# Rotary embedding on one core: fp32 tiles cast on ScalarE, against bf16 tiles of whole batch rows cast inside GpSimd-queue DMAs

## The chip, the cores and the metric

One core of a Trainium2 chip. The metric is device time in microseconds (us) of the whole program. Engines: DVE is VectorE, ACT is ScalarE, POOL is GpSimd, SP is SyncE; in the traces, DMAs issued from SP are queue q1, from ACT q10 and from GpSimd q0 (software_dynamic, here the software queue), all booked on the same 16 DMA engines (before: q1 50.1% and q10 49.1% of their span). SBUF is the memory of the kernel's tiles. A packet is one record of the DMA trace; here, but for small records of 4 bytes, it is one contiguous row of DRAM (in the kernel before, 29 DMAs of 128 rows of 32 KB are 3712 records).

## The reference

```python
# x: (8, 2048, 16, 64) fp32; cos, sin: (2048, 32) fp32
x1, x2 = x_pairs[..., 0], x_pairs[..., 1]      # neighbouring elements
out1 = x1 * cos - x2 * sin
out2 = x1 * sin + x2 * cos
out  = stack([out1, out2], axis=-1)            # fp32
```

x and out have 67.1 MB each, the two tables 0.5 MB together. So at least 134.7 MB cross the DMA engines, and each element needs three elementwise operations: multiply by sin, multiply by cos, add with the neighbours swapped.

## The kernel before

There are 16 tiles of 128 partitions x 8 seq rows x 1024 elements in fp32 (32 KB per partition, 4 MB per tile), in 5 buffers. ACT casts half a tile to bf16, DVE does three bf16 `tensor_tensor` operations, and ACT casts back to fp32 into the same tile. Loads are issued from SP, stores from ACT. The first and the last tile are cut into smaller runs.

```python
def load(i):
    g, b = groups[i]
    tiles[i] = xpool.tile([P, K, HD], fp32, name="xt")            # 5 buffers
    for k0, k1 in load_runs(i):
        nc.sync.dma_start(out=tiles[i][:, k0:k1], in_=x_t[b, g, :, k0:k1])

def halve(j):
    i, k0, k1 = pieces[j]
    halved[j] = hpool.tile([P, 4, HD], bf16, name="xh", bufs=3)
    nc.scalar.copy(out=halved[j][:, : k1 - k0], in_=tiles[i][:, k0:k1])
# ... rotate(j): three nc.vector.tensor_tensor in bf16 ...
def widen(j):
    i, k0, k1 = pieces[j]
    nc.scalar.copy(out=tiles[i][:, k0:k1], in_=rotated.pop(j)[:, : k1 - k0])
    # ... nc.scalar.dma_start(out=out_t[...], in_=tiles[i][...]) when the tile is complete
    if k1 == K and i + NX < n:
        load(i + NX)                       # SP waits until the store of tile i has landed
```

## Time and profile before

| | before |
|---|---|
| time, median of the runs beside the change | 318.56 us |
| span of the profiled run | 316.93 us |
| DVE busy / ACT busy | 223.2 / 230.0 us |
| bytes read and written in DRAM | 134.7 MB |
| share of 16 DMA engines' span filled by packets of the two big queues | 99.2% |

The profile's page of the kernel before: span; busy time with its share of the span; the busy tenths of each engine in 40 slices and what the DMA engines moved; the queues with packets, MB and share of 16 engines' span; the chain that ended last; then the groups of instructions (busy us, mean ns, idle time before them and what ended it).

```profile
span 316.9 us, 352 instructions
DVE 223.2 (70%) x111; ACT 230.0 (73%) x73; POOL 0.2 (0%) x4
...
DVE  0189999999999596693967939588440999999112
ACT  4078899999998692976949679495803999997322
...
DMA  7999999999999999999999999999999999999997
...
DMA packets 6451, 134.76 MB, mean 425 GB/s; under 512 B 689, under 2 KB 1201, under 8 KB 1969
...
q1 hardware_dynamic: 3712, 67.63, 50.1%
q10 hardware_dynamic: 2736, 67.11, 49.1%
...
HBM read 67.63 MB, written 67.11 MB: 425 GB/s over the span
...
DMA 62%; ACT 26%; DVE 4%; issue 3%; another core or an unknown queue 2%; SPq 1%; ACTq 1%
...
L75 ACT CAST xh<-xt 128x4096 bf16<-128x4096 f32 (+2 forms) x36 | 116.1, 3224 | 66.9 <-DMA xt<-in_x_dram 61.6
L105 ACT CAST xt<-xh 128x4096 f32<-128x4096 bf16 (+2 forms) x36 | 116.0, 3223 | 14.8 <-DVE xh L100 14.4
L94 DVE TENSOR_TENSOR qt<-xh,s_tab 128x4096 bf16<-128x4096 bf16 (+2 forms) x36 | 74.0, 2055 | 71.2 <-ACT xh L75 70.3
...
L121 DVE CAST s_tab<-sin_sb 128x512 bf16<-128x512 f32 x1 | 0.5, 453 | 14.4 <-DMA sin_sb<-in_sin_dram 14.4
```

Both compute engines are idle for over a quarter of the span, and what they wait for leads back to loads. The DMA row is 9 from the second slice to the last but one. That ACT holds 26% of the chain that ended last does not make it a bound: the chain walks through one instruction at a time, and during nearly every ACT cast on it the DMA engines were full as well.

The trace's packet records are sharper than the slices: 27.2 bytes per ns is the slope between the 16 KB packet (611 ns) and the 32 KB packet (1213 ns), loads and stores alike. 134.74 MB at 16 x 27.2 bytes/ns take 309.6 us. So the kernel before spends only 7.3 us of its span on anything but moving bytes at that rate.

### The profile page before, as it was taken

How to read it: one execution, taken by the hardware profiler on the slowest of the kernel's cores; microseconds unless marked ns; L12 is line 12 of the kernel's file. 1: busy time of each engine (PE TensorE's matmuls, PEld its weight loads, DVE VectorE, ACT ScalarE, POOL GpSimd, SP SyncE). 2: the span in 40 equal slices, each digit the busy share in tenths (PEclk: the TensorE clock that was granted, in tenths of full speed). 3: DMA queues.
4: the chain of work that ended last, by engine and by line, in shares of the span. 5: the costliest groups of instructions: out<-in, count | busy, mean ns of one | idle time of the engine just before them, and what ended most of it. 6: DMA issues, size and time to landing. Idle time of an engine off the chain costs nothing.

```text
span 316.9 us, 352 instructions
## 1 busy us (share of the span) xinstructions
DVE 223.2 (70%) x111; ACT 230.0 (73%) x73; POOL 0.2 (0%) x4
## 2 busy tenths in 40 slices
DVE  0189999999999596693967939588440999999112
ACT  4078899999998692976949679495803999997322
POOL 0000000000000000000000000000000000000000
DMA  7999999999999999999999999999999999999997
GB/s 304 424 463 405 455 397 401 459 438 422 455 405 463 397 460 401 459 414 448 443 418 455 405 459 405 455 405 459 418 443 447 414 428 430 424 433 439 442 414 302
DMA packets 6451, 134.76 MB, mean 425 GB/s; under 512 B 689, under 2 KB 1201, under 8 KB 1969
## 3 DMA queue, kind: packets, MB, share of 16 engines
q1 hardware_dynamic: 3712, 67.63, 50.1%
q10 hardware_dynamic: 2736, 67.11, 49.1%
q14 instruction: 3, 0.02, 0.0%
HBM read 67.63 MB, written 67.11 MB: 425 GB/s over the span
## 4 chain that ended last, share of the span: by engine, by line
DMA 62%; ACT 26%; DVE 4%; issue 3%; another core or an unknown queue 2%; SPq 1%; ACTq 1%
DMA xt<-in_x_dram 31%; DMA out_dram<-xt 28%; ACT xt L105 14%; ACT xh L75 12%; DMA sin_sb<-in_sin_dram 4%; DVE xh L100 1%; DVE xh L95 1%; DVE qt L94 1%; SPq L70 1%; ACTq L109 1%; DVE s_tab L121 0%; SPq L115 0%; DVE s_tab L122 0%; ACTq L105 0%
## 5 line engine op out<-in xcount | busy, mean ns | idle before, releaser
L75 ACT CAST xh<-xt 128x4096 bf16<-128x4096 f32 (+2 forms) x36 | 116.1, 3224 | 66.9 <-DMA xt<-in_x_dram 61.6
L105 ACT CAST xt<-xh 128x4096 f32<-128x4096 bf16 (+2 forms) x36 | 116.0, 3223 | 14.8 <-DVE xh L100 14.4
L94 DVE TENSOR_TENSOR qt<-xh,s_tab 128x4096 bf16<-128x4096 bf16 (+2 forms) x36 | 74.0, 2055 | 71.2 <-ACT xh L75 70.3
L100 DVE TENSOR_TENSOR xh<-xh,qt 128x4096 bf16<-128x4096 bf16 (+2 forms) x36 | 74.0, 2055 | 1.2
L95 DVE TENSOR_TENSOR xh<-xh,c_tab 128x4096 bf16<-128x4096 bf16 (+2 forms) x36 | 74.0, 2055 | 1.2
L121 DVE CAST s_tab<-sin_sb 128x512 bf16<-128x512 f32 x1 | 0.5, 453 | 14.4 <-DMA sin_sb<-in_sin_dram 14.4
L75 ACT ACT_TABLE_LOAD x1 | 1.3, 1283 | 0.7 <-PEq L147 0.7
L123 DVE CAST c_tab<-cos_sb 128x1024 bf16<-128x1024 f32 x1 | 0.7, 684 | 0.0
L122 DVE TENSOR_SCALAR s_tab<-sin_sb 128x512 bf16<-128x512 f32 x1 | 0.4, 442 | 0.0
L147 POOL MEMSET const-bfloat16-1.0<- 128x1 bf16 x1 | 0.1, 101 | 0.0
L147 POOL MEMSET const-uint8-127<- 128x1 uint8 x1 | 0.1, 101 | 0.0
L147 POOL MEMSET const-float32-0.0<- 128x1 f32 x1 | 0.1, 98 | 0.2 <-issue 0.2
L147 POOL MEMSET const-float32-1.0<- 128x1 f32 x1 | 0.1, 98 | 0.0
## 6 DMA issues: line engine op xcount, KB each, us to landing
out_dram<-xt ACTq DMA_DIRECT2D x15, 4096.0 KB, 38.6
xt<-in_x_dram SPq DMA_DIRECT2D x14, 4096.0 KB, 26.6
xt<-in_x_dram SPq DMA_DIRECT2D x2, 2048.0 KB, 16.3
xt<-in_x_dram SPq DMA_DIRECT2D x4, 512.0 KB, 24.1
xt<-in_x_dram SPq DMA_DIRECT2D x2, 1024.0 KB, 19.9
out_dram<-xt ACTq DMA_DIRECT2D x1, 2048.0 KB, 17.6
out_dram<-xt ACTq DMA_DIRECT2D x1, 1024.0 KB, 11.7
out_dram<-xt ACTq DMA_DIRECT2D x2, 512.0 KB, 4.1
```

The source lines that it names most:

```text
L70: nc.sync.dma_start(out=tiles[i][:, k0:k1], in_=x_t[b, g, :, k0:k1])
L75: nc.scalar.copy(out=halved[j][:, : k1 - k0], in_=tiles[i][:, k0:k1])
L94: nc.vector.tensor_tensor(out=rows(qt), in0=rows(xh), in1=tab(s_tab), op=mult)
L95: nc.vector.tensor_tensor(out=rows(xh), in0=rows(xh), in1=tab(c_tab), op=mult)
L100: nc.vector.tensor_tensor(out=xh3, in0=xh3, in1=q_swap, op=add)
L105: nc.scalar.copy(out=tiles[i][:, k0:k1], in_=rotated.pop(j)[:, : k1 - k0])
L109: nc.scalar.dma_start(out=out_t[b, g, :, r0:r1], in_=tiles[i][:, r0:r1])
L121: nc.vector.tensor_copy(out=s2[:, :, 0], in_=sin_flat)
L122: nc.vector.tensor_scalar_mul(s2[:, :, 1], sin_flat, -1.0)
L123: nc.vector.tensor_copy(out=c_tab.rearrange("p g k (i j) -> p (g k i) j", j=2), in_=cos_sb.rearrange("p g c -> p (g c)").to_broadcast([P, ...
L147: nc = _bacc.Bacc("TRN2", target_bir_lowering=False, num_devices=1)
```

## The change

The intent: 64 KB DRAM rows instead of 32 KB, hence fewer packets, with halved tiles, so that five of them take as much of SBUF as before, and no casts on ACT. One tile is a batch (128 partitions x 16 seq rows), held in bf16 (32 KB per partition, 5 buffers as before). A load DMA reads fp32 and writes bf16, a store DMA reads bf16 and writes fp32; both are issued from GpSimd. The first 1 MB (HEAD) and the last 2 MB (TAIL) stay fp32 DMAs on SP with a cast on ACT.

```diff
-    K = 8
-    G = S // (P * K)
+    K = S // P              # 16
+    KP = 4
+    HEAD = 2
+    TAIL = 4
...
+    def load(b, k0=0):
+        if b not in tiles:
+            tiles[b] = xpool.tile([P, K, HD], bf16, name="xt")
+        nc.gpsimd.dma_start(out=tiles[b][:, k0:], in_=x_t[b, :, k0:])
+
+    def store(b, k1=K):
+        nc.gpsimd.dma_start(out=out_t[b, :, :k1], in_=tiles[b][:, :k1])
... (halve and widen are gone; rotate works in place on the tile, 4 rows at a time)
+        head = stage.tile([P, TAIL, HD], fp32, name="st")
+        for k in range(HEAD):
+            nc.sync.dma_start(out=head[:, k : k + 1], in_=x_t[0, :, k : k + 1])
         nc.sync.dma_start(out=cos_sb, in_=cos_t)
         nc.sync.dma_start(out=sin_sb, in_=sin_t)
+        load(0, HEAD)
+        for b in range(1, NX):
+            load(b)
...
+        for b in range(B):
+            ... # rotate the pieces of batch b
+            if b < B - 1:
+                store(b)
+            if b >= 1 and b - 1 + NX < B:
+                load(b - 1 + NX)          # one batch later than it could be
+        store(B - 1, K - TAIL)
+        tail = stage.tile([P, TAIL, HD], fp32, name="st")
+        # one element into batch 6's tile: waits until batch 6's store has landed
+        nc.scalar.copy(out=tiles[B - 2][:1, 0, :1], in_=tiles[B - 1][:1, K - 1, :1])
+        nc.scalar.copy(out=tail, in_=tiles[B - 1][:, K - TAIL :])
+        nc.sync.dma_start(out=out_t[B - 1, :, K - TAIL :], in_=tail)
```

More of the change, by code (lines that the diff above doesn't have):

```diff
@@ L31 @@
     NX = 5
-    x_t = x.rearrange("b (g p k) h d -> b g p k (h d)", p=P, k=K)
-    out_t = out.rearrange("b (g p k) h d -> b g p k (h d)", p=P, k=K)
-    cos_t = cos.rearrange("(g p k) c -> p g (k c)", p=P, k=K)
-    sin_t = sin.rearrange("(g p k) c -> p g (k c)", p=P, k=K)
+    HEAD = 2
+    TAIL = 4
+    x_t = x.rearrange("b (p k) h d -> b p k (h d)", p=P, k=K)
+    out_t = out.rearrange("b (p k) h d -> b p k (h d)", p=P, k=K)
+    cos_t = cos.rearrange("(p k) c -> p (k c)", p=P, k=K)
+    sin_t = sin.rearrange("(p k) c -> p (k c)", p=P, k=K)
@@ L39 @@
     consts = ctx.enter_context(tc.tile_pool(name="consts", bufs=1))
     xpool = ctx.enter_context(tc.tile_pool(name="xpool", bufs=NX))
-    hpool = ctx.enter_context(tc.tile_pool(name="hpool", bufs=1))
-    cos_sb = consts.tile([P, G, K * D2], fp32)
-    sin_sb = consts.tile([P, G, K * D2], fp32)
-    c_tab = consts.tile([P, G, K, D], bf16)
-    s_tab = consts.tile([P, G, K, D], bf16)
-    groups = [(g, b) for g in range(G) for b in range(B)]
-    n = len(groups)
-    first_runs = [(0, 1), (1, 2), (2, 4), (4, 8)]
@@ L51 @@
-    last_runs = [(0, 4), (4, 6), (6, 7), (7, 8)]
-    def load_runs(i):
-        return first_runs if i == 0 else last_runs if i == n - 1 else [(0, K)]
-    def store_runs(i):
-        return last_runs if i == n - 1 else [(0, K)]
-    pieces = []
-    for i in range(n):
-        runs = first_runs if i == 0 else last_runs if i == n - 1 else [(0, 4), (4, 8)]
-        pieces += [(i, k0, k1) for k0, k1 in runs]
-    tiles, halved, rotated = {}, {}, {}
-    def load(i):
-        g, b = groups[i]
-        tiles[i] = xpool.tile([P, K, HD], fp32, name="xt")
-        for k0, k1 in load_runs(i):
-            nc.sync.dma_start(out=tiles[i][:, k0:k1], in_=x_t[b, g, :, k0:k1])
@@ L72, in halve @@
-    def halve(j):
-        i, k0, k1 = pieces[j]
-        halved[j] = hpool.tile([P, 4, HD], bf16, name="xh", bufs=3)
-        nc.scalar.copy(out=halved[j][:, : k1 - k0], in_=tiles[i][:, k0:k1])
-    def rotate(j):
-        i, k0, k1 = pieces[j]
-        g, _ = groups[i]
+    qpool = ctx.enter_context(tc.tile_pool(name="qpool", bufs=1))
+    stage = ctx.enter_context(tc.tile_pool(name="stage", bufs=1))
+    cos_sb = consts.tile([P, K * D2], fp32)
+    sin_sb = consts.tile([P, K * D2], fp32)
+    c_tab = consts.tile([P, K, D], bf16)
@@ L80, in rotate @@
+    s_tab = consts.tile([P, K, D], bf16)
+    tiles = {}
+    def load(b, k0=0):
[4 more added lines that the diff above has]
+        nc.gpsimd.dma_start(out=out_t[b, :, :k1], in_=tiles[b][:, :k1])
+    def rotate(b, k0, k1):
         nk = k1 - k0
-        xh = halved.pop(j)
-        qt = hpool.tile([P, 4, HD], bf16, name="qt")
+        xp = tiles[b][:, k0:k1]
+        qt = qpool.tile([P, KP, HD], bf16, name="qt")
@@ L84, in rows @@
         def rows(a):
-            return a[:, :nk].rearrange("p k (h e) -> p k h e", h=H, e=D)
+            return a.rearrange("p k (h e) -> p k h e", h=H, e=D)
         def tab(a):
             return dataclasses.replace(
-                a,
-                offset=a.offset + (g * K + k0) * D,
-                ap=[a.ap[0], [D, nk], [0, H], [1, D]],
-            )
-        nc.vector.tensor_tensor(out=rows(qt), in0=rows(xh), in1=tab(s_tab), op=mult)
-        nc.vector.tensor_tensor(out=rows(xh), in0=rows(xh), in1=tab(c_tab), op=mult)
+                a, offset=a.offset + k0 * D, ap=[a.ap[0], [D, nk], [0, H], [1, D]]
+            )
@@ L96, in rotate @@
+        nc.vector.tensor_tensor(out=rows(qt[:, :nk]), in0=rows(xp), in1=tab(s_tab), op=mult)
+        nc.vector.tensor_tensor(out=rows(xp), in0=rows(xp), in1=tab(c_tab), op=mult)
         q_swap = dataclasses.replace(
@@ L98, in rotate @@
         )
-        xh3 = xh[:, :nk].rearrange("p k (a j) -> p (k a) j", j=2)
-        nc.vector.tensor_tensor(out=xh3, in0=xh3, in1=q_swap, op=add)
-        rotated[j] = xh
-    def widen(j):
-        i, k0, k1 = pieces[j]
-        nc.scalar.copy(out=tiles[i][:, k0:k1], in_=rotated.pop(j)[:, : k1 - k0])
-        g, b = groups[i]
-        for r0, r1 in store_runs(i):
-            if r1 == k1:
-                nc.scalar.dma_start(out=out_t[b, g, :, r0:r1], in_=tiles[i][:, r0:r1])
-        if k1 == K and i + NX < n:
-            load(i + NX)
+        x3 = xp.rearrange("p k (a j) -> p (k a) j", j=2)
@@ L113 @@
+        nc.vector.tensor_tensor(out=x3, in0=x3, in1=q_swap, op=add)
     with tc.manual_schedule():
-        load(0)
+        head = stage.tile([P, TAIL, HD], fp32, name="st")
+        for k in range(HEAD):
+            nc.sync.dma_start(out=head[:, k : k + 1], in_=x_t[0, :, k : k + 1])
         nc.sync.dma_start(out=cos_sb, in_=cos_t)
         nc.sync.dma_start(out=sin_sb, in_=sin_t)
-        for i in range(1, NX):
-            load(i)
-        s2 = s_tab.rearrange("p g k (i j) -> p (g k i) j", j=2)
@@ L120 @@
-        sin_flat = sin_sb.rearrange("p g c -> p (g c)")
-        nc.vector.tensor_copy(out=s2[:, :, 0], in_=sin_flat)
-        nc.vector.tensor_scalar_mul(s2[:, :, 1], sin_flat, -1.0)
+        load(0, HEAD)
+        for b in range(1, NX):
+            load(b)
+        nc.scalar.copy(out=tiles[0][:, :HEAD], in_=head[:, :HEAD])
+        s2 = s_tab.rearrange("p k (i j) -> p (k i) j", j=2)
+        nc.vector.tensor_copy(out=s2[:, :, 0], in_=sin_sb)
+        nc.vector.tensor_scalar_mul(s2[:, :, 1], sin_sb, -1.0)
@@ L123 @@
         nc.vector.tensor_copy(
-            out=c_tab.rearrange("p g k (i j) -> p (g k i) j", j=2),
-            in_=cos_sb.rearrange("p g c -> p (g c)").to_broadcast([P, G * K * D2, 2]),
-        )
-        halve(0)
-        for j in range(len(pieces)):
-            if j + 1 < len(pieces):
-                halve(j + 1)
-            rotate(j)
-            widen(j)
+            out=c_tab.rearrange("p k (i j) -> p (k i) j", j=2),
+            in_=cos_sb.to_broadcast([P, K * D2, 2]),
+        )
+        for b in range(B):
+            if b == 0:
+                rotate(b, 0, HEAD)
+                rotate(b, HEAD, KP)
+            for k0 in range(KP if b == 0 else 0, K, KP):
+                rotate(b, k0, k0 + KP)
+            if b < B - 1:
+                store(b)
+            if b >= 1 and b - 1 + NX < B:
+                load(b - 1 + NX)
```

## The prediction

> **What bounds the kernel now.** The DMA engines. In the page's 40 slices the DMA row is 9 in all but the two end slices. The DMA table gives 134.76 MB at a mean of 425 GB/s; packets of the load queue (50.1%) and the store queue (49.1%) fill 99.2% of 16 engines' span. A 32 KB packet, load or store, takes 1213 ns, a 16 KB one 611 ns: 27.2 bytes per ns and about 8 ns fixed. [...] Counted over time, the engines lose only 4.1 us of 316.9 us, half at each end. In the view of waits DVE waits 70.3 us for ACT, ACT 61.6 us for loads.
>
> **What the change does.**
> - It removes nearly all casts from ACT (230 us busy). They are 26% of the chain of waits, but DMA runs full at the same time, so I count about 0 us for this.
> - DVE work stays: about 32 pieces x 3 x 2.29 us, 223 us.
> - DMA bytes on the DRAM side stay at 134.7 MB; on the SBUF side they are halved. I take it that a cast packet costs what its wider side costs: the engine must still read 4 bytes per element in a load and write 4 in a store at 27.2 bytes/ns, and loads and stores follow each other in one queue in 8 MB blocks, so the idle half of each isn't overlapped.
> - Rows of 64 KB instead of 32 KB: estimate 2409 + 8 ns, against 2 x 1213. Saves about 1.1 us per engine.
> - Estimate per engine: head in 4 KB packets (16 x 159 ns) 2.5 us, cos/sin 1.3, loads 152.3, stores 154.7: 311 us busy, against 312.8 now.
> - Start: head and tables (3.8 us of transfers) cover the start of the software-generated queue. End: the last 6 MB (48 KB rows) and 2 MB (16 KB rows) have 128 rows each in two queues, which end together if they alternate. DVE should be done by about 255 us.
> - [...]
>
> Together: 311 us of transfers + 2 at each end + 1.6 from span to time = 316 us, 0.8% faster.
>
> **What would show it.** DMA row full from end to end; 64 KB packets near 2.42 us in loads and stores; DVE 223 us busy and 90 us idle, waiting for loads; ACT nearly empty; GpSimd's stores long from issue to landing, queued behind loads.
>
> **What would make it wrong.**
> 1. Cast packets priced by the SBUF side or the mean of both: well under 2.4 us per 64 KB. DMA would fall to 160-235 us and DVE (223 us, plus start, last cast and store) would bound it at 240-255 us; a partial gain gives 260-305.
> 2. Cast packets dearer than plain ones: 330 us and beyond.
> 3. Bubbles in the single queue: a load waits for a store of the same buffer to land; with another store queued behind, I expect none.
> 4. An end not balanced between the queues: a few us.
>
> 80% range 292 to 325. Faster by over 2% 0.27, within 2% 0.57, slower by over 2% 0.16.

The sum: 311 + 2 + 2 + 1.6 us, 316.4 with the 310.8 behind the 311, which the text gives as 316; its 1.6 is time less span of the kernel before (318.5 - 316.9). Of the start, the changed kernel's trace shows SP's first packet at 1.7 us, 1.0 us after its issue, and its head packets until 6.0 us; GpSimd's first packet came at 5.1 us, 3.9 us after its issue. Of the end it shows turns of one 16 KB packet (644 ns) and one of the 48 KB rows (1828 ns), but only from 305.8 us on: the GpSimd queue's data ended at 311.1 us, SP's at 314.8.

## The result and the profile after

| | before | after |
|---|---|---|
| time, median | 318.56 us | 317.54 us |
| ratio | | 0.9967, 95% interval 0.995 to 0.9985 |
| span of the profiled run | 316.93 us | 316.01 us |
| ACT busy | 230.0 us | 6.9 us |
| DVE busy | 223.2 us | 221.8 us |

A ratio is the mean time of one kernel's runs over that of the other's in the same rounds, so it is not quite the ratio of the medians. The change is 1.0 us faster where 2.5 us were forecast. Nearly all work of an engine was removed and the time moved by a third of a per cent.

The page of the changed kernel, the same parts, with the DMA issues at its end (KB each on the SBUF side, median us from issue to landing).

```profile
span 316.0 us, 198 instructions
DVE 221.8 (70%) x102; ACT 6.9 (2%) x4; POOL 8.9 (3%) x20
...
DVE  0000039999999999999999999999999999100000
ACT  1200000000000000000000000000000000000400
...
DMA  9899999999999999999999999999999999999996
...
DMA packets 3025, 101.72 MB, mean 322 GB/s; under 512 B 336, under 2 KB 336, under 8 KB 848
...
q0 software_dynamic: 2304, 98.04, 96.8%
q1 hardware_dynamic: 720, 3.67, 3.1%
...
HBM read 67.63 MB, written 67.11 MB: 426 GB/s over the span
...
another core or an unknown queue 91%; DMA 2%; ACTq 1%; ACT 1%; SPq 0%; issue 0%
...
L94 DVE CAST s_tab<-sin_sb 128x512 bf16<-128x512 f32 x1 | 0.5, 453 | 44.2 <-DMA sin_sb<-in_sin_dram 44.2
...
L117 ACT CAST st<-xt 128x4096 f32<-128x4096 bf16 x1 | 3.6, 3599 | 0.0
...
out_dram<-st SPq DMA_DIRECT2D x1, 2048.0 KB, 15.5
st<-in_x_dram SPq DMA_DIRECT2D x2, 512.0 KB, 4.5
cos_sb<-in_cos_dram SPq DMA_DIRECT2D x1, 256.0 KB, 22.4
sin_sb<-in_sin_dram SPq DMA_DIRECT2D x1, 256.0 KB, 42.1
```

How to read it:

- The DMA row is as full as before. The mean of 322 GB/s is a trap: a cast load is recorded with the bytes that it wrote (bf16; 32 KB for a 64 KB row). The line with DRAM bytes shows the true rate, 426 GB/s, as before (425).
- The view of the chain is of no use here. It does not know the GpSimd queue's landings and books 91% as an unknown queue. Packet records carry the argument instead.
- The cast packets cost what their wide side costs. From the packet records (median ns):

```text
packet                            before      after
32 KB fp32 -> 32 KB fp32          1213        -
64 KB fp32 -> 32 KB bf16 (load)   -           2432
32 KB bf16 -> 64 KB fp32 (store)  -           2449
```

So a halved SBUF side buys nothing: 64 KB take 2432 ns in a cast load, 2449 ns in a cast store and 2 x 1213 = 2426 ns in two plain ones. That premise of the prediction held, in loads and in stores.

Recorded durations of neighbouring packets overlap a little (in the changed kernel 64 KB cast loads of 2432 ns start 2413 ns apart on an engine, in the median), so their sums are not exact. A better account is the time in which the engines did not move bytes: for each stretch of the span, its length less (DRAM-side bytes moved in it) / (16 x 27.2 bytes/ns), a cast load counted with twice its recorded bytes. In us:

```text
stretch of the span        0-20   20-100   100-260   260-310   310-end   sum
before                     2.95    1.02     0.81      0.39      2.15     7.32
after                      3.22    0.50     0.57      0.12      1.99     6.40
```

The middle is 1.0 us better, the start 0.3 us worse, the end 0.2 us better. That is the difference of the two spans, 0.9 us.

One thing in the profile was not foreseen. DVE starts at 44 us, not near 10: the sin table, 256 KB, needs 42.1 us from issue to landing. Its packets (2 KB, 96 ns) share each DMA engine with the GpSimd queue's packets, and the records show turn-taking: one 2 KB packet, then one of 2129 or 2431 ns, and so on, with 16 table packets per engine. The 256 table packets start in 16 rounds of 16, about 2204 ns apart beside the packets of 2129 ns and 2505 ns apart beside those of 2431 ns. DVE's end moved too, to 269.4 us, where I had expected 255. DVE's idle time is 44.2 us before the table and 46.6 us after its last piece; the view of waits names no wait for loads. Whether that costs time is tested below.

### The profile page after: what moved, and what is told of

Read it like the earlier page. It is cut to its first block, busy times and chain, and to the rows that moved or that the text cites. A ratio compares the mean times of both kernels' runs of the same rounds, so it can differ in the third digit from the quotient of the medians.

```text
span 316.0 us, 198 instructions
## 1 busy us (share of the span) xinstructions
DVE 221.8 (70%) x102; ACT 6.9 (2%) x4; POOL 8.9 (3%) x20
## 4 chain that ended last, share of the span: by engine, by line
another core or an unknown queue 91%; DMA 2%; ACTq 1%; ACT 1%; SPq 0%; issue 0%
DMA st<-in_x_dram 2%; ACTq L144 1%; ACT xt L92 1%; ACT L92 0%; SPq L85 0%; ACT xt L116 0%; ACTq L116 0%; ACTq L92 0%
## 5 line engine op out<-in xcount | busy, mean ns | idle before, releaser
L75 DVE TENSOR_TENSOR xt<-xt,c_tab 128x4096 bf16<-128x4096 bf16 (+1 forms) x33 | 73.5, 2228 | 1.1
L80 DVE TENSOR_TENSOR xt<-xt,qt 128x4096 bf16<-128x4096 bf16 (+1 forms) x33 | 73.5, 2228 | 1.1
L74 DVE TENSOR_TENSOR qt<-xt,s_tab 128x4096 bf16<-128x4096 bf16 (+1 forms) x33 | 73.5, 2228 | 1.1
L94 DVE CAST s_tab<-sin_sb 128x512 bf16<-128x512 f32 x1 | 0.5, 453 | 44.2 <-DMA sin_sb<-in_sin_dram 44.2
L59 POOL DMA_DIRECT2D out_dram<-xt x8 | 4.3, 535 | 202.1 <-DVE xt L80 202.1
L56 POOL DMA_DIRECT2D xt<-in_x_dram x8 | 4.4, 561 | 52.1 <-DMA out_dram<-xt 51.3
L117 ACT CAST st<-xt 128x4096 f32<-128x4096 bf16 x1 | 3.6, 3599 | 0.0
L92 ACT CAST xt<-st 128x2048 bf16<-128x2048 f32 x1 | 1.9, 1899 | 0.0
## 6 DMA issues: line engine op xcount, KB each, us to landing
sin_sb<-in_sin_dram SPq DMA_DIRECT2D x1, 256.0 KB, 42.1
```

The source lines that it names most:

```text
L56: nc.gpsimd.dma_start(out=tiles[b][:, k0:], in_=x_t[b, :, k0:])
L59: nc.gpsimd.dma_start(out=out_t[b, :, :k1], in_=tiles[b][:, :k1])
L74: nc.vector.tensor_tensor(out=rows(qt[:, :nk]), in0=rows(xp), in1=tab(s_tab), op=mult)
L75: nc.vector.tensor_tensor(out=rows(xp), in0=rows(xp), in1=tab(c_tab), op=mult)
L80: nc.vector.tensor_tensor(out=x3, in0=x3, in1=q_swap, op=add)
L92: nc.scalar.copy(out=tiles[0][:, :HEAD], in_=head[:, :HEAD])
```

## The experiments

Theory A: the DMA engines are full, a cast packet pays its wide side, so only fixed costs per packet and the two ends can change; the gain is the longer rows. Rivals: the gain comes from freeing ACT or from the single queue (B); only cast packets become cheaper with length (C). Sixteen further runs were made, one of them a repetition of the changed kernel. Each is compared by its ratio to the kernel before of the same rounds; the changed kernel stands at 0.9967, and at 0.9962 in its repetition.

### The row length

**rows32**: every cast DMA cut into two of 32 KB DRAM rows.

```diff
-        nc.gpsimd.dma_start(out=tiles[b][:, k0:], in_=x_t[b, :, k0:])
+        for r0, r1 in ((k0, 8), (8, K)):
+            nc.gpsimd.dma_start(out=tiles[b][:, r0:r1], in_=x_t[b, :, r0:r1])
```

and the same for `store`.

> The changed kernel with every 64 KB DRAM row cut into two of 32 KB (two DMAs per batch and direction), cast and queue kept. Theory A (the whole gain is fewer packets: 2412.5 ns per 64 KB cast row against 2 x 1210 ns in the kernel before): gain vanishes, 318.4 to 318.7 us, cast packets at a pitch of about 1210 ns per 32 KB. Rival B (gain from taking ACT off the way or from the single queue): stays at 317.4 to 317.7 us. Rival C (the cast makes a packet a little cheaper): in between.

Measured: 319.47 us, ratio 1.0024 (1.0012 to 1.0036), 1.9 us slower than the changed kernel, more than any theory said. The trace shows a fault of the experiment: the dummy copy that holds back the tail now waited for only one half of batch 6's store. So the tail began 9 us early, SP finished its data at 310.3 us and the GpSimd queue ended last, at 315.2 us, 2.4 us before the span's end. In the changed kernel the last data came from SP, 1.2 us before the end.

**rows32_end**: the same, with the dummy copy waiting for the other half.

```diff
-        nc.scalar.copy(out=tiles[B - 2][:1, 0, :1], in_=...)
+        nc.scalar.copy(out=tiles[B - 2][:1, K - 1, :1], in_=...)
```

> rows32 again, but the dummy copy that holds the fp32 tail back waits for the second half of batch 6's store instead of the first, so that the SyncE tail again ends last, as in the changed kernel. Theory D (32 KB rows cost only 0.3 to 0.5 us; the rest of rows32's 1.9 us came from its end, where the GpSimd queue ended last and its completion came 2.4 us after its last data packet, against 1.2 us of the SyncE queue): 317.8 to 318.2 us. Rival A (the rows are worth 1 us or more): 318.5 to 319.5 us.

Measured: 318.82 us, ratio 1.0001 (0.9989 to 1.0013). That is the rival's number, not D's. With 32 KB rows the changed kernel ties with the kernel before, so ACT and the single queue are worth little together (against B): at most what the other end and the cut rows hide. In the trace the middle lost only 0.3 us to the changed kernel, the end 0.45 us, so the end was still another one, and 0.2 us lie outside the span (see below). A cleaner cut was needed.

**after_again, rows32_mid, rows16_mid**: the changed kernel as control, and rows cut only in the loads of batches 1 to 7 and the stores of batches 0 to 5, so that start and end stay as they are.

```diff
+        kr = 8 if b else K              # rows16_mid: 4
+        for r in range(k0 if b else 0, K, kr):
+            r0 = max(r, k0)
+            nc.gpsimd.dma_start(out=tiles[b][:, r0 : min(r + kr, K)], in_=...)
```

> The changed kernel unchanged, as the control for the other three of these rounds: 317.3 to 317.8 us.

> The changed kernel with 64 KB rows cut into two of 32 KB in the loads of batches 1 to 7 and the stores of batches 0 to 5 only (104 rows per engine); head, first load, last two stores and tail as they are. Theory F (about 6 ns fixed per cast packet, from pitches of 2411 ns per 64 KB and 1208.4 ns per 32 KB in two earlier traces): +0.6 us over after_again. Rival A (rows are worth the whole difference of rows32_end, 1.3 us): +1.0 us or more.

> The same with four rows of 16 KB each. Theory F: three more packets of 6 ns per 64 KB, 104 rows: +1.9 us over after_again, three times the effect of rows32_mid. Rival A: +3 us. If it is no multiple of rows32_mid, the cost isn't per packet.

Measured: 317.60 us (ratio 0.9962), 318.18 us (0.9983, 0.997 to 0.9995) and 319.01 us (1.0009, 0.9995 to 1.0023). By the medians, +0.58 and +1.41 us over the control. Per added packet that is 0.58 us / 104 = 5.6 ns and 1.41 us / 312 = 4.5 ns: a little under theory F's 6 ns, and not the rival's.

One thing makes rows32_mid less sure. The time of a run is longer than its core's span by 1.93 to 2.05 us in rows32, rows32_end and rows32_mid, and by 1.75 to 1.79 us in all other kernels (means of the runs). So 0.3 us of rows32_mid's loss lie outside the span; why, the record does not show. By the spans' means rows32_mid is 0.36 us and rows16_mid 1.50 us over the control, 3.5 and 4.8 ns per added packet. Three times the packets cost 2.4 times as much by the medians and 4.2 times by the spans, so a constant cost per packet is not cleanly shown, but its size is: 3.5 to 5.6 ns. Over all 128 rows of an engine these make 0.4 to 0.7 us. Unfilled time in the stretch from 100 to 260 us, which in the changed kernel and its variants has nothing but cast packets, agrees (0.25 us for about 66 added packets, 4 ns each):

```text
                  before   after_again   rows32_mid   rows16_mid   copy64   copy32
unfilled, us       0.81       0.54          0.79         1.44       0.79     0.72
```

The row length is therefore about 0.4 to 0.7 of the 1.05 us gained.

**copy64, copy32**: a plain fp32 copy, wrong result, no compute; loads on SP, stores on ACT, with 64 KB or 32 KB rows.

```diff
+    def load(b):
+        tiles[b] = xpool.tile([P, K, HD], fp32, name="xt")        # 3 buffers of 64 KB
+        for k in range(0, K, ROWS):                               # ROWS = 16 or 8
+            nc.sync.dma_start(out=tiles[b][:, k : k + ROWS], in_=x_t[b, :, k : k + ROWS])
```

> Wrong result on purpose: only copies x to out in fp32, no compute, no tables, loads on SyncE and stores on ACT, 64 KB rows. Theory A: 64 KB per packet pitch 2412 ns without any cast, so about 1 us less than copy32; about 315 us in all. Rival C (only the cast packets gain): no difference from copy32.

> The same copy with 32 KB rows (two DMAs per batch and direction): Theory A: pitch 1210 ns per 32 KB, about 1 us more than copy64, near 316 us. Rival C: the same time as copy64.

Measured: copy32 316.88 us (316.64 to 318.04). copy64 316.61 us in its profiled run and 319.6 to 320.6 us in the five others, and I have no trace of a long one; as a comparison of times the pair is inconclusive. The two traces show no saving: a plain 64 KB packet takes 2418 ns, but starts follow each other in 2420 ns, twice 1210, and the unfilled time above is 0.79 against 0.72 us. In these traces plain packets from SP and ACT gain nothing from going beyond 32 KB, cast packets from GpSimd do (C). No run has plain 64 KB packets from GpSimd, so it stays open whether the cast or the queue makes this difference. copy32 is also a floor: with no compute and no tables, this traffic takes 316.9 us. No kernel that moves these bytes in this way has much left to gain.

### Can the idle half of a cast packet be used?

**interleave**: for the three steps that have both a store and a load, cut them into 8 DMAs of 16 partitions and alternate.

```diff
+                for p in range(0, P, PI):            # PI = 16
+                    for k in range(0, K, KI):        # KI = 16
+                        s = (slice(p, p + PI), slice(k, k + KI))
+                        nc.gpsimd.dma_start(out=out_t[b][s], in_=tiles[b][s])
+                        nc.gpsimd.dma_start(out=tiles[nb][s], in_=x_t[nb][s])
```

> The changed kernel; for the three steps that have both a store and a load (batches 1 to 3 out, 5 to 7 in), the two 8 MB DMAs are cut into 8 DMAs of 16 partitions each, and store and load slices alternate in the queue[...]. Premise of the prediction (a cast packet costs its wider side and the idle half of it is not overlapped with its neighbour): 317.4 to 318.2 us, 64 KB pitch 2.41 us. Rival (the reading and the writing half of an engine run apart, so a load's narrow write overlaps a store's wide write of the next row): up to 9.6 us less for each of the three steps, 288 to 310 us.

Measured: 360.12 us, ratio 1.13. Neither. The load packets of the stage grew from 2432 to about 3600 ns, the stores from 2449 to about 3000 ns. Why the packets grew no run shows. The experiment could not answer its question.

**interleave_k**: the same with slices over all partitions and 2 seq rows (PI = 128, KI = 2, 8 KB DRAM rows).

> interleave again without its fault: the slices are now 2 of the 16 seq rows over all 128 partitions (8 KB DRAM rows), store and load slices alternating, so every engine gets 64 KB of store, 64 KB of load, and so on[...]. Premise (the wide side of each packet is paid in full): 8 KB rows cost about 2% more than 64 KB rows on the 48 MB that are cut, 319 to 321 us. Rival (the narrow side of one packet overlaps the wide side of the next): clearly below 315 us, down to 290.

Measured: 321.09 us, ratio 1.0074 (1.0061 to 1.0087), just above the premise's 319 to 321 and far from the rival's. An 8 KB cast packet took 324 ns as a load and 341 ns as a store (medians), although 64 KB of loads and 64 KB of stores alternated on every engine; 8 KB at 27.2 bytes/ns are 301 ns. With overlap a pair would have taken well under 602 ns. Over the stage the engines moved bytes at 98% of 27.2 bytes/ns each (0.8 us unfilled in each 40 us from 140 to 220 us), never above it. So the wide side is paid in full in this arrangement; finer alternation was not tried.

### The queue itself

**pool_plain**: the kernel before, with its 4 MB fp32 DMAs issued from GpSimd.

```diff
-            nc.sync.dma_start(out=tiles[i][:, k0:k1], in_=...)
+            q = nc.sync if i == 0 else nc.gpsimd
+            q.dma_start(out=tiles[i][:, k0:k1], in_=...)
...
-                nc.scalar.dma_start(out=out_t[b, g, :, r0:r1], in_=...)
+                nc.gpsimd.dma_start(out=out_t[b, g, :, r0:r1], in_=...)
```

> The kernel before with all its 4 MB fp32 loads and stores (but the first) issued from GpSimd instead of SyncE and ACT; no cast, rows still 32 KB. Theory A: same as before, 318.3 to 318.8 us, unless loads and stores in one queue make bubbles. Rival B (a single software-generated queue has a smaller pitch): 317.4 to 317.8 us. If the software queue is dearer: over 319 us.

**pool_lag**: the same with each load issued one tile later, behind the next store.

```diff
-        if k1 == K and i + NX < n:
-            load(i + NX)
+        if k1 == K and i >= 1 and i - 1 + NX < n:
+            load(i - 1 + NX)
```

> pool_plain with each load issued one tile later, behind the next store, as the changed kernel does, so that GpSimd never waits with an empty queue. Plain fp32, 32 KB rows, software queue. Theory E (pool_plain's 389 us came from waiting with nothing queued, not from the queue itself): 318.5 to 320.5 us, a little dearer at the end than the kernel before. Rival (the software queue is slow for plain rows): stays over 340 us.

Measured: 389.38 us (ratio 1.2216) and 353.85 us (1.1102). The view of waits of pool_plain, then of pool_lag (engine, line and what it waited for; us in total, times, longest):

```profile
POOL xt L71 <- DMA out_dram<-xt: 235.1, 11, 23.0
```

```profile
POOL out_dram L110 <- ACT xt L106: 164.0, 12, 71.6
POOL xt L71 <- DMA out_dram<-xt: 142.6, 9, 19.4
DVE s_tab L122 <- DMA sin_sb<-in_sin_dram: 53.3, 1, 53.3
```

And pool_lag by stretches (busy us and instructions of DVE, ACT and POOL; clock; DMA share; GB/s):

```profile
20.00:40.00 20.00, 0.00 (x0) 0.00 (x0) 0.00 (x0) 1.00 1.02 437
40.00:60.00 20.00, 5.75 (x10) 3.20 (x3) 0.00 (x0) 1.00 0.61 257
60.00:100.00 40.00, 38.19 (x19) 38.20 (x13) 1.60 (x3) 1.00 0.51 210
100.00:140.00 40.00, 38.82 (x18) 39.97 (x12) 2.65 (x5) 1.00 1.00 419
140.00:180.00 40.00, 33.24 (x15) 34.25 (x11) 2.12 (x4) 1.00 1.00 430
```

In pool_plain, GpSimd waits for a store to land before it issues the load into the same buffer (235.1 us in all), and meanwhile the next finished store cannot be issued from the same program. The lag removes 36 us of that, so theory E had part of the cause. Its number missed, because the late tables come back here with a price: DVE starts at 53 us, the five loads issued in advance are only 20 MB, no data moves from 52 to 76 us, and by 100 us the engines have lost 28 us more than in the kernel before. (This reading rests on the waits and stretches of one trace; pool_lag with early tables was not run.) From 100 us on the DMA share is 1.00. The software queue is not slow for plain rows (its 32 KB packets take 1213 ns, as in the kernel before); what it cost was its place in a program that waits. The changed kernel is safe from both: its loads lag, and its five tiles in advance hold 40 MB, which last until about 100 us (its first store packet starts at 101.2 us).

### The late tables

**tables_first**: cos and sin before the head on SP. **tables_pool**: cos and sin from GpSimd, ahead of its first load.

```diff
-        nc.sync.dma_start(out=cos_sb, in_=cos_t)
-        nc.sync.dma_start(out=sin_sb, in_=sin_t)
+        nc.gpsimd.dma_start(out=cos_sb, in_=cos_t)
+        nc.gpsimd.dma_start(out=sin_sb, in_=sin_t)
         load(0, HEAD)
```

(tables_first moves the two SP lines above the head instead.)

> The changed kernel with cos and sin issued on SyncE before the 1 MB head instead of behind it. Both theories: DVE's first table cast starts near 8 to 15 us instead of 44.2 us, and DVE ends its last piece earlier, about 240 to 260 us instead of 269 us. Theory (DMA-bound, DVE's late start costs nothing): 317.2 to 317.8 us as before. Rival (the 44 us of idle DVE matter): 1 us or more faster.

> The changed kernel with cos and sin issued from GpSimd ahead of the first 7 MB load, so that nothing stands between them in turn-taking. DVE's first table cast at 6 to 12 us instead of 44.2 us, DVE ends earlier. Theory (DMA is the bound from end to end, 35 us of idle DVE cost nothing): 317.2 to 317.9 us. Rival: at least 1 us faster.

Measured for tables_first: 318.26 us, ratio 0.9983 (0.9965 to 1.0001), its runs spread from 317.27 to 319.47. The expectation for DVE missed: the tables were there at 4.1 us, but now the head's 4 KB packets were the ones that took turns, ACT waited 45.8 us for them, and DVE's first multiplication began at 49.0 us (45.5 in the changed kernel) and its last piece ended at 272.9 us, not at 240 to 260. The starvation had only changed its victim.

Measured for tables_pool: 317.80 us, ratio 0.9968 (0.9954 to 0.9981). Its waits and its DVE row:

```profile
DVE qt L74 <- DMA xt<-in_x_dram: 32.7, 3, 11.2
DVE s_tab L94 <- DMA sin_sb<-in_sin_dram: 7.6, 1, 7.6
```

```profile
DVE  0508999999999999999999980799708996000000
```

DVE starts at 7.6 instead of 44.2 us, then waits 32.7 us for loads, and the time is that of the changed kernel. In this kernel the late DVE costs nothing.

### The ends

**no_head**: no fp32 head, batch 0 is one cast load. **no_tail**: batch 7 is one cast store, no cast on ACT. **head8**: the head as one DMA of 8 KB rows instead of two of 4 KB rows.

```diff
-        for k in range(HEAD):                                   # no_head: removed
-            nc.sync.dma_start(out=head[:, k : k + 1], in_=x_t[0, :, k : k + 1])
+        nc.sync.dma_start(out=head[:, :HEAD], in_=x_t[0, :, :HEAD])    # head8
...
-        store(B - 1, K - TAIL)                                  # no_tail
+        store(B - 1)                                            # and the tail removed
```

> The changed kernel without the 1 MB fp32 head: SyncE carries only the tables at the start, batch 0 is one cast load of 8 MB. The first GpSimd packet came at 3.5 us where the tables led; the tables (1.5 us of transfer from 1.75 us on) nearly cover that. Theory: 317.4 to 318.2 us, so the head is worth under 0.7 us. Rival (the software queue starts late and the head saves its whole delay of 3.4 us): 319.5 to 321 us.

> The changed kernel with the last 2 MB stored like the rest: one cast DMA of 8 MB for batch 7, no ACT cast, no SyncE store. Theory D (a GpSimd cast DMA completes about 1.2 us later after its last packet than a SyncE one, nothing else changes): 318.5 to 319.2 us. Rival (the tail is worth nothing, since DMA is full anyway): 317.3 to 317.8 us.

> The changed kernel with the 1 MB head loaded by one DMA of 8 KB rows instead of two of 4 KB rows. Theory G (the first packets of the run are slow: mean 209 ns against 159 ns for 4 KB; fewer and larger ones lose less): 0.2 to 0.5 us less than after_again, and the unfilled share of the first 10 us falls from 3.1 to about 2.7 us. Rival: the loss is the first microseconds after the queue starts, whatever the packet: no change.

Measured: no_head 319.55 us (1.0018, 1.0005 to 1.003); no_tail 318.02 us (0.9978, 0.9965 to 0.9991); head8 317.70 us (0.9965, 0.9953 to 0.9978).

no_tail is about 0.4 us slower than the changed kernel, between D's number and the rival's, and with overlapping intervals. Its trace ends 1.8 us after the GpSimd queue's last data packet, the changed kernel's 1.2 us after SP's.

no_head is about 1.6 us slower by the ratios, more than the theory and less than the rival. Its profiled run was its fastest (318.64 us). Even there the start was no worse (3.24 us unfilled to 20 us, against 3.22); it lost 0.4 us more between 20 and 140 us and 0.5 us more at the end. Why the head is worth what it is stays open.

head8 answered as theory G at the start and as its rival in the time. Unfilled time of the first 10 us fell from 3.08 to 2.58 us, but between 60 and 140 us it rose from 0.47 to 1.42 us. Both traces have a disturbance there, in the last load packets before the kernel's first store: 16 packets slower by 1.2 us per engine in head8, 14 slower by 0.3 us in after_again. The half microsecond won at the start was gone by then.

## Why the prediction was wrong

The time lies in the stated range and within 2%, and the main mechanism held. The forecast gain of 2.5 us did not come: it was 1.05 us (1.02 by the medians, 0.33% of 318.6 by the ratio). Point by point:

- **"a cast packet costs what its wider side costs"**: right. 2432 and 2449 ns per 64 KB against 2 x 1213; alternating loads and stores did not overlap (interleave_k).
- **Casts on ACT "about 0 us"**: right within about half a microsecond. With 32 KB rows the changed kernel ties with the kernel before (1.0001) though ACT is empty.
- **DVE "223 us busy and 90 us idle"**: right in size (221.8 and 94), wrong in the wait: not "waiting for loads", but 44.2 us for the sin table and 46.6 us after its last piece. "DVE should be done by about 255 us" was wrong, 269.4 us. The late tables are not all of it: in tables_pool, with the table at 7.6 us, DVE waits for loads and still ends at 266.0 us. That run also shows that the late DVE cost nothing.
- **"I expect none" (bubbles)**: right. The stretches from 20 to 310 us have 1.2 us unfilled together.
- **"311 us busy, against 312.8 now"**: this is the step that failed. Counted alike, as the time in which the engines have a packet in flight (the mean of at most 16 at once), the trace of the changed kernel has 311.9 us and that of the kernel before 312.9 us: 1.0 us saved where the step has 2.0 (310.8 before rounding). "2 at each end" held (4.1 us in all). Two terms of the step were mis-sized, the next two points.
- **"Saves about 1.1 us per engine" (rows)**: I took 8 ns per packet from recorded durations, which overlap; the runs show 3.5 to 5.6 ns per added packet, 0.4 to 0.7 us.
- **"head in 4 KB packets (16 x 159 ns) 2.5 us, cos/sin 1.3"**: the largest error. Their packets took 3.3 and 1.5 us per engine in the trace, 1.1 us more by these records, mostly because many of the run's first packets are slow (mean 209 ns, up to 1053 ns, where 159 ns is the steady value: 0.8 us per engine). The kernel before pays such a start too (its first 4 KB packets took 191 ns in the mean: 0.5 us), and that loss was inside my measured "312.8 now". So the step set steady prices on one side against measured ones on the other, and booked the start's slowness as a saving.
- **The sum**: 310.8 + 2 + 2 + 1.6 is 316.4, and the text rounded it to 316. This is another 0.4 us of the forecast gain.

Together: at the prediction's own prices (27.2 bytes/ns and 8 ns per packet) for both kernels, with 360 packets of data per engine before and 168 after, the transfers would have been 312.5 against 310.9 us, a saving of about 1.5 us. So about 0.5 of the 2.0 us came from mixing two kinds of price and from rounding. The other 0.5 us are the 8 ns and the start, which is slower in the changed kernel (0.8 against 0.5 us per engine); how they share it is an estimate at best.

What remains of the measured 1.05 us after the rows is 0.35 to 0.65 us. Of the 192 packets that the change saves per engine only 128 are due to the row length; the other 64 are small ones, of the tables and of the cut first and last tiles. At 3.5 to 5.6 ns each they would bring 0.2 to 0.4 us, an estimate that no run tests. In one pair of traces some of it lies in the load packets just before the first store (0.6 us extra per engine in the kernel before at 36 to 40 us, 0.3 us in the changed one at 98 to 100 us). As this differs between runs and variants, what remains is not settled.

## What to carry to other kernels

Here packets filled the DMA engines from end to end, and a cast inside the DMA did not lighten them: 64 KB of fp32 took 2432 ns as a cast load and 2449 ns as a cast store, against 2418 ns as a plain packet, and 223 us of work taken off ACT were worth no more than about half a microsecond. So count the wider side, and expect little of freed compute. A forecast of one part in three hundred must price both kernels in the same way, measured start against measured start. And small DMAs that compute needs first should go ahead of the big ones in the same queue: beside another queue's large packets the sin table got one turn per packet here and took 42.1 us to land, ahead of them in the same queue 5.6 us (tables_pool). The delay was harmless here while enough loads were in flight (ratio 0.9967 with it, 0.9968 without).
